# Order ties in a two-layer GLA and attention kernel: row maxima, attention set-up, prompt keys, last rows

## The chip, the cores and the metric

The kernel runs on one core of a Trainium2 chip. The metric is the device time of one execution in microseconds (us); the time before is the median of three runs, 1268.66 us (1267.31 to 1269.15).

## What is computed

Two layers of a diffusion backbone, D = 1024, on 256 prompt tokens and 1024 latent tokens. Layer 0 mixes tokens with bidirectional gated linear attention (GLA), layer 1 with grouped-query softmax attention (8 query heads, 2 key heads, head size 128). Cut to what matters here:

```
out_p, st = gla_mixer(hp, ...);  out_s, _ = gla_mixer(hs, ...)      # layer 0
xp = xp + gt_p * out_p;          xs = xs + gt_s * out_s
qp, kp, vp, gp = attn_project(hp, ...)                              # layer 1: q, k are rms-normed
out_p = (attend_blocks(qp, kp, vp) * silu(gp)) @ att_w_out          # prompt rows see prompt keys
qs, ks_ = rope_2d(qs), rope_2d(ks_)
out_s = (attend_blocks(qs, keys, vals) * silu(gs)) @ att_w_out      # latent rows: own keys and cached ones
xp = xp + gt_p * out_p;          xs = xs + gt_s * out_s
return xp, xs, gla state, prompt keys kp, prompt values vp
```

## The kernel before, in words

The 1280 tokens are ten rows of 128: rows 0 and 1 are the prompt, rows 2 to 9 the latent tokens. A product in full precision is made of three f16 products: each operand is split into a high and a low part (names hi, lo), and TensorE (PE) runs hi.hi, hi.lo and lo.hi into one PSUM bank (`pieces` and `mm3`, all at L135). Before a split the operand is scaled by a power of two that comes from its largest magnitude (`pow2`, L98 to L108: a reduction or a row maximum, then four tiny VectorE (DVE) operations).

A scheduler orders the instructions of each engine, so the code's order is not the order on the chip. `tc.issue_after(x)` ties what stands under it behind instruction x. Engines take their instructions strictly in the order so made; a wait at the head holds up all behind it.

The stages that the change touches:

- **Last GLA slots** (`filler` in the main function, slots 40 to 49). `row_load` fetches a row of GLA output from DRAM (`og_d` to `wst` or `wlo`); `row_parts` takes its maximum (L931), scales and splits it (ScalarE (ACT) L934 high part, DVE L935 low part), and a transposing DMA (L937) puts it into `hT_hi` and `hT_lo`, from which PE reads it. `row_out` makes the output row from the banks A and kt: `residual` (L916 scales the bank by the gate, L917 adds the residual row). The rows are made in the order `ROWS = (2, 3, 4, 5, 6, 7, 8, 9, 0, 1)`, the first six in the slots `EARLY = (43, 44, 45, 46, 47, 49)`. `fold_gate` loads the gate and multiplies it on GpSimd (POOL) with the weights' scales.
- **gla_out**. The last four rows (8, 9, 0, 1) are made in two banks y, and between them rows are normed (`normalise`: ACT L434 sums the squares, DVE L440 scales), transposed on PE (L445), and turned into keys and values (`key_tile`). `att_load` and `att_setup` load and scale the norm weights and the cached keys; `fill` (`out_part`) takes the attention's output weights, whose block maxima are DVE L157. Loads are issued on the SP queue.
- **key_tile** makes 128 rows of keys and values: PE product, ACT L1128 and L1131, `head_norm` (ACT L1026 twice, POOL L124 and L126, DVE L1029 twice), rotary positions for latent rows only, `split_transpose` (ACT L1056, DVE L1057, a transposing DMA L1058). For prompt rows the normed key is stored to the output cache (L1134).
- **attention**: ten steps (two key heads, five groups of 256 rows, `OUT = (1, 0, 2, 3, 4)` in the second half) of four heads each. `scores` runs PE L1180 into a tile S, takes the maximum (DVE L1183), makes its bias (ACT L1185) and the exponentials (ACT L1188), then the split (POOL L1204, DVE L1220) and a transposing DMA (L1221) to `PT`; two tiles S alternate, so that the third scores wait for the exponentials of the first. `values` multiplies with the values and the gate (DVE L1245). In the last step the first output rows are prepared.
- **att_out**: for each group of 256 rows `out2_load` fetches the gated result, `out2_scale` takes its maximum (DVE L1335 twice, L1339, PE L93, DVE L98 to L108), `out2_parts` splits it (ACT L1346, DVE L1347, in two halves of k), and `out_tile` runs two residual rows of 24 matmuls 512 wide and 48 matmuls 256 wide each (L916, L917, and a store L919). The residual row is loaded in `out_tile` (L1355).

## Time and profile before

| | |
|---|---|
| median of three runs | 1268.66 us |
| the profiled execution's own time | 1266.46 us |
| its span, first to last instruction | 1264.7 us (1.76 us lie outside) |
| mean granted TensorE clock | 0.995 |
| PE busy | 1212.7 us, 8310 matmuls |
| DVE, ACT, POOL busy | 887.0, 593.2, 402.0 us |

PE is the engine that everything else feeds. Where PE waits, the list of waits names the line that waited, the instruction that released it, the time in total, how often and the longest. A timeline row gives start, duration, engine, line, operation with output and inputs, and in square brackets the idle time of that engine just ahead of it with what ended it. A row of windows gives the busy time of PE, PEld (weight loads), DVE, ACT and POOL in a stretch, the granted PE clock (PEclk), the share of the DMA engines in use and GB/s.

### The profile page before, as it was taken

To read this page: it belongs to the slowest core of one execution; us is meant where nothing else is said; L and a number is where in the kernel's file an instruction comes from. 1 tells how busy PE (TensorE), PEld (TensorE's weight loads), DVE (VectorE), ACT (ScalarE), POOL (GpSimd) and SP (SyncE) were. 2 spreads that over 40 slices of the span, in tenths; PEclk is the share of its full clock that TensorE was granted. 3 is DMA by queue.
4 is the path that set the end of the run, shared out by engine and by line. 5 is a ranking of instruction groups with operands and counts; after the bars stand their busy time and mean duration, and the time that the engine had idled before them with its cause. 6 is when DMAs were issued, how large, how long until landed. Compare 5 with 4: busy or idle time off the path is not lost.

```text
span 1264.7 us, 22661 instructions
## 1 busy us (share of the span) xinstructions
PE 1212.7 (96%) x8310; PEld 810.4 (64%) x8310; DVE 887.0 (70%) x2040; ACT 593.2 (47%) x1439; POOL 402.0 (32%) x659
## 2 busy tenths in 40 slices
PE   5999999999999998989899989999999999999998
PEld 2448666655565556656688757767776766776665
DVE  5665886776688898763577678777658577795552
ACT  5564555555466666320255554444445355451010
POOL 0022222232233233300034645545344365533000
PEclk9999999999999999999999999999999999999999
DMA  9621365543444436893943166766938647668432
GB/s 356 208 101 35 109 196 151 188 146 113 128 124 137 129 113 215 262 207 112 333 151 118 26 163 154 137 139 134 213 80 201 141 92 149 134 159 214 163 124 93
DMA packets 335840, 194.42 MB, mean 154 GB/s; under 512 B 229662, under 2 KB 318606, under 8 KB 334448
## 3 DMA queue, kind: packets, MB, share of 16 engines
q1 hardware_dynamic: 293664, 159.02, 46.9%
q10 hardware_dynamic: 42064, 33.95, 8.3%
q8 instruction: 65, 1.06, 0.4%
q14 instruction: 47, 0.39, 0.1%
HBM read 103.00 MB, written 33.83 MB: 108 GB/s over the span
## 4 chain that ended last, share of the span: by engine, by line
PE 67%; DVE 14%; DMA 8%; ACT 4%; POOL 3%; issue 3%; SPq 0%; POOLq 0%; ACTq 0%; DVEq 0%
PE mm L135 35%; PE S L1180 7%; PE S L135 7%; PE A L135 2%; PE kt L135 2%; DVE wmx L157 2%; PE y L135 2%; DMA wst<-og_d 2%; PE kv L135 2%; PE A L750 2%; DMA wst<-in_gla_w_in 1%; DVE split L239 1%; POOL rope L1040 1%; DVE smx L1183 1%; PE A L691 1%
## 5 line engine op out<-in xcount | busy, mean ns | idle before, releaser
L135 PEld LDWEIGHTS <-hT_hi 128*128 128x128 f16 x1920 | 188.1, 98 | 133.6 <-issue 12.9
L135 PE MATMUL mm<-whi,hT_hi 128*128 128x512 f16 (+1 forms) x560 | 195.1, 349 | 4.3 <-DVE gx L280 2.5
L135 PE MATMUL mm<-whi,hT_lo 128*128 128x512 f16 (+1 forms) x560 | 195.3, 349 | 0.0
L135 PE MATMUL mm<-wlo,hT_hi 128*128 128x512 f16 (+1 forms) x560 | 195.2, 349 | 0.0
L135 PEld LDWEIGHTS <-whi 128*128 128x128 f16 x1344 | 131.3, 98 | 49.9 <-issue 2.9
L1204 POOL TENSOR_SCALAR phl<-p,srec 128x1280 f16<-128x1280 f32 (+1 forms) x80 | 105.4, 1317 | 167.8 <-DVE srec L1200 130.8
L1183 DVE TENSOR_REDUCE smx<-S 128x1 f32<-128x1280 f32 (+1 forms) x80 | 101.7, 1271 | 50.7 <-PE S L1180 50.7
L135 PEld LDWEIGHTS <-hT_lo 128*128 128x128 f16 x960 | 94.3, 98 | 62.1 <-issue 2.9
L135 PE MATMUL mm<-hT_hi,whi 128*128 128x256 f16 (+1 forms) x448 | 131.1, 293 | 0.0
L135 PE MATMUL mm<-hT_hi,wlo 128*128 128x256 f16 (+1 forms) x448 | 131.1, 293 | 0.0
L135 PE MATMUL mm<-hT_lo,whi 128*128 128x256 f16 (+1 forms) x448 | 131.0, 292 | 0.0
L1180 PE MATMUL S<-kT,wst 128*128 128x512 f16 (+1 forms) x624 | 122.1, 340 | 3.7 <-ACT p L1188 3.7
L1220 DVE SCALAR_TENSOR_TENSOR phl<-p,srec,phl 128x1280 f16<-128x1280 f32 (+1 forms) x80 | 107.6, 1345 | 15.0 <-POOL phl L1204 14.7
L135 PE MATMUL mm<-PT,vh 128*128 128x256 f16 x672 | 112.2, 273 | 1.8 <-DVE wlo L1347 1.2
L1188 ACT ACTIVATE p<-S,snb,sexp 128x1280 f32<-128x1280 f32 (+1 forms) x80 | 99.7, 1246 | 14.6 <-DVE phl L1220 5.2
L1180 PEld LDWEIGHTS <-wst 128*128 128x128 f16 x624 | 61.2, 98 | 54.8 <-issue 4.9
L135 PE MATMUL mm<-PT,vl 128*128 128x256 f16 x336 | 91.6, 273 | 0.0
L135 PEld LDWEIGHTS <-wlo 128*128 128x128 f16 x672 | 66.0, 98 | 24.3 <-issue 0.3
L1185 ACT ACTIVATE snb<-smx,nsexp 128x1 f32<-128x1 f32 x80 | 23.5, 293 | 110.1 <-DVE smx L1183 109.6
L135 PEld LDWEIGHTS <-vh 128*128 128x128 f16 x672 | 65.6, 98 | 10.5 <-issue 1.7
L1040 POOL TENSOR_TENSOR rope<-hx,ropet 128x64 f32<-128x64 f32 x160 | 66.2, 442 | 15.4 <-DVE hx L1043 10.3
L157 DVE TENSOR_REDUCE wmx<-wst 128x1 f32<-128x512 f32 x96 | 60.4, 674 | 7.4 <-DMA wst<-in_gla_w_in 7.4
(391 smaller groups left out, 2586.1 us busy)
## 6 DMA issues: line engine op xcount, KB each, us to landing
wada<-in_w_ada SPq DMA_DIRECT2D x13, 1024.0 KB
wst<-in_gla_w_in SPq DMA_DIRECT2D x12, 1024.0 KB
wst<-in_att_w_in SPq DMA_DIRECT2D x10, 1024.0 KB
xr<-x_d SPq DMA_DIRECT2D x15, 512.0 KB
og_d<-qk ACTq DMA_DIRECT2D x40, 128.0 KB
wst<-og_d SPq DMA_DIRECT2D x5, 1024.0 KB
out<-xr ACTq DMA_DIRECT2D x17, 256.0 KB
x<-in_x_sample SPq DMA_DIRECT2D x8, 512.0 KB
```

The source lines that it names most:

```text
L135: self.nc.tensor.matmul(out, a, b, start=k == 0 and j == 0, stop=k == n - 1 and j == 2)
L157: nc.vector.tensor_reduce(mx[:, j : j + 1], st[:, 2 * j : 2 * j + 2, :], AX.XY, ALU.max, apply_absolute_value=True)
L239: nc.vector.scalar_tensor_tensor(t[:, 1, v], u, s, t[:, 0, v], ALU.mult, ALU.subtract)
L691: nc.tensor.matmul(ap[:, d, :], ke[:, d, :], qe[:, d, :], start=True, stop=True)
L750: nc.tensor.matmul(o, x, y, start=j == 0, stop=j == len(terms) - 1)
L1040: nc.gpsimd.tensor_tensor(tv[:, h, :, w, :], xv[:, h, :, 1 - w, :], sn[:, :, w, :], ALU.mult)
L1180: nc.tensor.matmul(S[:, a : a + n], x, y, start=m == 0, stop=m == 2)
L1183: last = nc.vector.tensor_reduce(mx, S, AX.X, ALU.max).ins
L1185: nc.scalar.activation(nb, mx, AF.Copy, scale=self.nsexp)
L1188: nc.scalar.activation(p, S, AF.Exp, scale=self.sexp, bias=nb, accum_out=den)
L1204: nc.gpsimd.tensor_scalar(parts[:, 0:nk], p, r, 2.0 ** 14, ALU.mult, ALU.mult)
L1220: nc.vector.scalar_tensor_tensor(lo, p, r2, hi, ALU.mult, ALU.subtract)
```

## The change

It puts ties on the order at five places, and moves some work and two loads for them. Numbers of lines shift by 1 to 35 in the changed kernel (L916 and L917 become L924 and L925, L931 becomes L941, L1188 becomes L1209).

1. The maxima of rows 7, 8 and 9 stand behind the residual adds number 0, 2 and 3 (row 2 bank A, row 3 bank A, row 3 bank kt). The second half of `fold_gate` moves to slot 43.
2. The attention's set-up and the first block of output weights stand behind the last residual add of row 9.
3. A prompt row's keys stay in `qk0` after the product; their norm, store, split and transpose become `prompt_keys`, called after the first and the second scores and tied behind those scores' maxima.
4. The residual of the first output row is loaded earlier, in the last step, as two halves of 128x512 into the buffers that queries used (`hx4`), instead of one row of 128x1024 loaded in `out_tile`.
5. In `att_out` the scaling of the next group is tied behind an earlier residual add, or for the first one behind the first of the last values.

```diff
+BEHIND = {7: 0, 8: 2, 9: 3}
...
     def residual(self, i, lhs, wo, inv, x, banks=None, cuts=(512, 512), out=None):
+            xa = x[j] if isinstance(x, list) else x[:, a]
-            nc.vector.tensor_tensor(x[:, a], ps, x[:, a], ALU.add)
+            self.evac.append(nc.vector.tensor_tensor(xa, ps, xa, ALU.add).ins)
...
     def row_parts(self, i, parts):
+        n = BEHIND.get(i)
+        with nullcontext() if n is None else self.tc.issue_after(self.evac[n]):
+            mx = self.t(self.small, [P, 1], F32, "wm1")
+            nc.vector.tensor_reduce(mx, og, AX.X, ALU.max, apply_absolute_value=True)
...
-        with self.tc.issue_after(self.scaled):
+        with self.tc.issue_after(self.scaled), self.tc.issue_after(self.evac[-1]):
             self.att_setup(*ckv)
...
-        fill(0)
+        with self.tc.issue_after(self.evac[-1]):
+            fill(0)
...
     def key_tile(self, i, w):
-        x = self.t(self.hw, [P, 2, HD], F32, "hx")
+        if i < NTP:
+            x = self.qk0[:, 2048 + 256 * i : 2304 + 256 * i].rearrange("p (h d) -> p h d", h=2)
+        else:
+            x = self.t(self.hw, [P, 2, HD], F32, "hx")
-        self.head_norm(x, self.kn, x)
...
+            self.prompt.append((i, x))
         else:
+            self.head_norm(x, self.kn, x)
             self.rope(x, i)
...
+    def prompt_keys(self):
+        with self.tc.issue_after(self.last):
+            i, x = self.prompt.pop(0)
+            j = 10 + i
+            self.head_norm(x, self.kn, x)
+            self.nc.scalar.dma_start(self.O[3][0, 0, i * P : i * P + P], x)
+            self.split_transpose(x, self.asc[:, 1:2], self.kT[:, :, j * P : j * P + P])
...
                 if n == 9 and e == 0:
+                    self.first_values = None
+                    x0 = [self.t(self.hw, [P, 4, HD], F32, "hx4").rearrange("p h d -> p (h d)") for _ in range(2)]
+                    for b, t in enumerate(x0):
+                        self.nc.sync.dma_start(t, self.x1_d[2 * OUT[0], :, 512 * b : 512 * b + 512])
...
-        self.out_tile(OUT[0], 0, self.t(self.sp, [P, TS + PAST], F32, "p")[:, 0:D], wo)
+        self.out_tile(OUT[0], 0, x0, wo)
...
-                nxt = self.out2_prep(self.out2_load(OUT[n + 1]), to) if n else self.out2_parts(*self.second, to)
+                with self.tc.issue_after(self.evac[-1 - (n > 1)] if n else self.first_values):
+                    nxt = self.out2_prep(self.out2_load(OUT[n + 1]), to) if n else self.out2_parts(*self.second, to)
```

**How the order moves, place 1: DVE in the last GLA slots.** `wm` is a row's maximum, `A` and `kt` the banks of output row 3, `whi` here the buffer of its residual. Before, the maximum of row 8 and that of row 9 stand ahead of bank A's pair:

```order
L931 TENSOR_REDUCE wm_1850_7238<-wst_6294 128x1
L102 TENSOR_SCALAR p2c_7240<-wm_1850_7238 128x1
L104 TENSOR_SCALAR p2e_7242<-p2c_7240 128x1
L935 SCALAR_TENSOR_TENSOR wlo_1711_6414<-wlo_1711_6414,p2s_7101 128x1024
L106 TENSOR_SCALAR p2s_7244<-p2e_7242 128x1
L108 TENSOR_SCALAR p2i_7246<-p2e_7242 128x1
L931 TENSOR_REDUCE wm_1878_7401<-wst_6294 128x1
L916 SCALAR_TENSOR_TENSOR A_6811<-A_6811,p2i_6553,wst_6402 128x512
L98 TENSOR_REDUCE p2m_7266<-o_7264 128x1
L935 SCALAR_TENSOR_TENSOR parts_6295<-wst_6294,p2s_7244,parts_6295 128x1024
L917 TENSOR_TENSOR whi_1710_6413<-A_6811,whi_1710_6413 128x512
```

and now (what is left out are the tiny operations of row 8's scale and of the next layer's modulation):

```order
L945 SCALAR_TENSOR_TENSOR wlo_1711_6406<-wlo_1711_6406,p2s_7101 128x1024
L924 SCALAR_TENSOR_TENSOR A_6811<-A_6811,p2i_6545,wst_6402 128x512
L99 TENSOR_REDUCE p2m_7266<-o_7264 128x1
L925 TENSOR_TENSOR whi_1710_6405<-A_6811,whi_1710_6405 128x512
L941 TENSOR_REDUCE wm_1850_7238<-wst_6294 128x1
...
L945 SCALAR_TENSOR_TENSOR parts_6295<-wst_6294,p2s_7244,parts_6295 128x1024
L924 SCALAR_TENSOR_TENSOR kt_6812<-kt_6812,p2i_6545,wst_6402 128x512
L925 TENSOR_TENSOR whi_1710_6405<-kt_6812,whi_1710_6405 128x512
L941 TENSOR_REDUCE wm_1878_7401<-wst_6294 128x1
```

Both maxima have moved behind the adds that they are tied to, and the pair of bank A stands together but for one reduction.

**Place 2: DVE in gla_out, around row 9.** `y` is a bank of an output row, `xr` its residual, `st` a block of output weights, `nt` the norm's sums. Before:

```order
L1108 TENSOR_SCALAR sv_i_7905<-inv_av_7902 128x1
L124 TENSOR_SCALAR nt_r2a_7638<-nt_s_1928_7635 128x2
L440 TENSOR_SCALAR xr_7616<-xr_7616,nt_r_1930_7640 128x1024
L440 TENSOR_SCALAR xr_7618<-xr_7618,nt_r_1930_7640 128x1024
L916 SCALAR_TENSOR_TENSOR y_7670<-y_7670,p2i_7246,wst_6402 128x512
L157 TENSOR_REDUCE wmx_7992<-st_7632 128x1
L124 TENSOR_SCALAR nt_r2a_7780<-nt_s_1947_7777 128x2
L157 TENSOR_REDUCE wmx_7992<-st_7632 128x1 x3
L917 TENSOR_TENSOR xr_7620<-y_7670,xr_7620 128x512
```

and now:

```order
L1119 TENSOR_SCALAR sv_i_7905<-inv_av_7902 128x1
L125 TENSOR_SCALAR nt_r2a_7638<-nt_s_1928_7635 128x2
L924 SCALAR_TENSOR_TENSOR y_7670<-y_7670,p2i_7246,wst_6402 128x512
L441 TENSOR_SCALAR xr_7616<-xr_7616,nt_r_1930_7640 128x1024
L441 TENSOR_SCALAR xr_7618<-xr_7618,nt_r_1930_7640 128x1024
L925 TENSOR_TENSOR xr_7620<-y_7670,xr_7620 128x512
L125 TENSOR_SCALAR nt_r2a_7780<-nt_s_1947_7777 128x2
L441 TENSOR_SCALAR xr_7622<-xr_7622,nt_r_1949_7782 128x1024
L441 TENSOR_SCALAR xr_7624<-xr_7624,nt_r_1949_7782 128x1024
```

The four L157 left the space between the pair of bank y (now L924 and L925).

**Place 3: ACT from the last prompt keys to the first exponentials.** `hx` before and `qk` now hold the prompt row's keys, `xhl` their split, `p` the exponentials. Before:

```order
L1128 ACTIVATE hx_9268<-kv_9219,inv_k_7900 128x256
L1131 ACTIVATE vh_7898<-kv_9219,psv_7908 128x256
L1134 DMA out<-hx_9197 128x256
L1056 ACTIVATE xhl_9215<-hx_9197,asc_7890 128x256
L1026 ACTIVATE hjunk_9271,hssq_9270<-hx_9268 128x128
L1136 ACTIVATE pv_2188_9283<-kv_9219,inv_av_7902 128x256
L1026 ACTIVATE hjunk_9271,hssq_9270<-hx_9268 128x128
L1137 DMA out<-pv_2188_9283 128x256
L1134 DMA out<-hx_9268 128x256
L1056 ACTIVATE xhl_9286<-hx_9268,asc_7890 128x256
L1185 ACTIVATE snb_9329<-smx_9327,nsexp_7894 128x1
L1188 ACTIVATE p_9331,sden_9332<-S_9309,snb_9329,sexp_7892 128x1280
```

and now:

```order
L1142 ACTIVATE qk_7_82<-kv_9203,inv_k_7900 128x256
L1144 ACTIVATE vh_7898<-kv_9203,psv_7908 128x256
L1148 ACTIVATE pv_2177_9255<-kv_9203,inv_av_7902 128x256
L1149 DMA out<-pv_2177_9255 128x256
L1206 ACTIVATE snb_9297<-smx_9295,nsexp_7894 128x1
L1209 ACTIVATE p_9299,sden_9300<-S_9277,snb_9297,sexp_7892 128x1280
L1170 ACTIVATE hx_2191_9308<-mm_9309,inv_q_1977_7928 128x256
L1170 ACTIVATE hx_2191_9308<-mm_9309,inv_q_1978_7930 128x256
...
L1037 ACTIVATE hjunk_9383,hssq_9382<-qk_7_82 128x128 x2
...
L1206 ACTIVATE snb_9369<-smx_9367,nsexp_7894 128x1
L1209 ACTIVATE p_9371,sden_9372<-S_9357,snb_9369,sexp_7892 128x1280
```

The norm's sums (L1037, four of them on `qk`) and the splits moved from ahead of the first exponentials (L1209) to behind them; the sums on `qk` stand ahead of the second ones.

On SP, the 1 MB load `whi<-w_q` of the first query weights now stands right behind the first two loads of `w_kv` and ahead of the six loads `xr`; before it stood behind the transposes of row 0 (`parts`). One of the two 0.5 MB loads `wkv` goes the other way.

More of the change, by code (lines that the diff above doesn't have):

```diff
@@ L894, in gla, with fold_gate @@
                 w = nw
-    def fold_gate(self, l, inv, gt):
+    def fold_gate(self, l, inv, gt, later=False):
         nc = self.nc
@@ L901, in fold_gate, with fold_rest @@
             nc.sync.dma_start(gt[:, i, :], self.gt_d[l, i : i + 1, :].to_broadcast([P, D]))
+        if later:
+            return
+        self.fold_rest(inv)
+    def fold_rest(self, inv):
+        nc, gt = self.nc, self.gt
         for b in range(4):
@@ L975, in gla_out @@
                 nc.sync.dma_start(w[part], d[:, part, :, 256 * j : 256 * j + 256])
-        self.o1 = []
+        self.o1, self.prompt = [], []
         fill = self.out_part(2, self.kept2)
@@ L1298, in attention @@
                     self.query_rest()
+                if self.prompt:
+                    self.prompt_keys()
                 if len(pend) == 2:
@@ L1354, in out_tile @@
         i, a = 2 * c + j, slice(j * P, j * P + P)
-        self.nc.sync.dma_start(x, self.x1_d[i])
+        if not isinstance(x, list):
+            self.nc.sync.dma_start(x, self.x1_d[i])
         S = self.t(self.ps, [P, 1536], F32, "S")
@@ L1556, in emit @@
         wo, part, held, rows, parts, xs, waiting = [None] * 4, [], [], [], [], [], []
+        inv_wo = None
         def filler(slot):
+            nonlocal inv_wo
             if part:
@@ L1599, in filler @@
                 gt = k.t(k.wst, [P, KT, 256], F32, "wst").rearrange("p (i k) n -> p i (k n)", i=2)
-                k.fold_gate(0, [t[2] for t in wo], gt)
+                inv_wo = [t[2] for t in wo]
+                k.fold_gate(0, inv_wo, gt, True)
                 wo[:] = [(*k.w0[0:2], 512)] + [(hi, lo, 256) for hi, lo, _ in wo[2:]]
+            if slot == EARLY[0]:
+                k.fold_rest(inv_wo)
             n = slot - LATE
```

13 lines of the change are left out of this document (5 added, 8 removed).

## The prediction

> **What bounds the kernel now.** I read the page first, then the list of PE's waits, then timelines at each place.
>
> ```profile
> PE 1212.7 (96%) x8310; PEld 810.4 (64%) x8310; DVE 887.0 (70%) x2040; ACT 593.2 (47%) x1439; POOL 402.0 (32%) x659
> PE A L135 <- DVE p2c L102: 3.9, 1, 3.9
> PE y L135 <- DVE xr L917: 2.8, 1, 2.8
> PE S L1180 <- ACT p L1188: 2.7, 1, 2.7
> ...
> PE tr L445 <- DVE xr L440: 0.6, 1, 0.6
> ...
> PE S L135 <- DVE p L917: 1.7, 2, 1.1
> PE mm L135 <- DVE wlo L1347: 1.2, 1, 1.2
> ```
>
> PE is busy 96% of the span, so only its idle time can be won, and of that the second half of the program holds the rows above (the first four from 500 to 800 us, the last two from 1100 to the end). The profile's clock shows a second cost behind the long ones; the rows are the stretches behind the first three waits:
>
> ```profile
> 555.00:560.00 5.00, 1.06 (x7) 0.54 (x5) 4.49 (x14) 0.00 (x0) 0.00 (x0) 0.90 1.11 295
> 560.00:565.00 5.00, 5.00 (x20) 1.95 (x18) 2.88 (x6) 1.15 (x1) 0.00 (x0) 0.76 1.13 252
> ...
> 625.00:630.00 5.00, 3.03 (x16) 2.22 (x17) 5.00 (x14) 1.02 (x2) 1.19 (x3) 0.72 1.11 260
> 630.00:635.00 5.00, 5.00 (x43) 4.20 (x42) 1.91 (x5) 1.02 (x2) 1.07 (x2) 0.93 0.82 292
> ...
> 740.00:745.00 5.00, 5.00 (x31) 3.59 (x30) 3.80 (x7) 3.30 (x11) 4.67 (x9) 0.67 0.36 82
> ```
>
> Over ten us behind the first wait the granted clock misses (0.10 + 0.24) x 5 = 1.7 us, behind the second (0.28 + 0.07) x 5 = 1.75, behind the third 0.33 x 5 = 1.65. Some of that falls on idle time, so I count 1.5 for each. The 1.1 to 1.2 us waits at the end show no such dip.
>
> **Place 1, the row maxima.** DVE in the last GLA slots:
>
> ```profile
> 550.29 1.22 DVE L931 TENSOR_REDUCE wm<-wst 128x1 f32<-128x1024 f32 x1 [2.05 <-DMA wst<-og_d]
> ...
> 555.51 1.22 DVE L931 TENSOR_REDUCE wm<-wst 128x1 f32<-128x1024 f32 x1 [2.29 <-DMA wst<-og_d]
> 556.64 0.75 DVE L916 SCALAR_TENSOR_TENSOR A<-A,p2i,wst 128x512 f32<-128x512 f32 x1
> 557.50 1.27 DVE L935 SCALAR_TENSOR_TENSOR parts<-wst,p2s,parts 128x1024 f16<-128x1024 f32 x1
> 558.69 0.68 DVE L917 TENSOR_TENSOR whi<-A,whi 128x512 f32<-128x512 f32 x1
> ```
>
> PE waits 3.9 us for bank A of row 3. The maximum of row 9 (555.51) waits 2.29 us for its load in front of the pair L916, L917, although the bank needs neither, and the low part at 557.50 stands between the two. In the new order the low part of row 7 (1.27) comes where the maximum of row 8 stood: from about 550 to 551.3, then L916 with the reduction (0.86, from 556.64 to 557.50) and L917 (0.68) end near 552.8. PE got the bank when L917 ended, at 559.4, so it wanted it at 559.4 - 3.9 = 555.5: this wait goes. What is late next is bank kt, wanted 24 matmuls of 512 columns later. At place 4 rows show 24 matmuls of 256 columns in 2.61 us (0.109 each, so 0.215 for twice the width): at 560.7. Ahead of its pair stand the maximum of row 8 (1.22, to 554.0), its scale (0.9, the time from L98 to L1346 in the rows of place 5), ACT's high part (1.1, half of that L1346) and the low part (1.27), so the pair ends near 558.8; if the row's load is 2 us later than at 550.29, no later than 560.8. Removed 3.9 + 1.5 = 5.4; I keep 0.2 for kt: **-5.2** (bounds -3.9 if the dip comes from elsewhere, -5.4). The maxima of rows 8 and 9 come some 3 us later; the products of rows 4 to 7 lie between them and their use. Moving the second half of the gate's multiplication costs nothing: it is POOL work with no wait on it in the list.
>
> **Place 2, set-up behind row 9.**
>
> ```profile
> 618.44 1.06 ACT L434 ACTIVATE junk<-xr 128x1024 f16<-128x1024 f32 x1 [12.22 <-DMA hT_lo<-parts]
> ...
> 623.78 0.68 DVE L157 TENSOR_REDUCE wmx<-st 128x1 f32<-128x512 f32 x1
> 624.44 1.87 DVE L157 TENSOR_REDUCE wmx<-st 128x1 f32<-128x512 f32 x3
> 626.23 0.68 DVE L917 TENSOR_TENSOR xr<-y,xr 128x512 f32<-128x512 f32 x1
> ...
> 605.00:610.00 5.00, 5.00 (x36) 3.24 (x34) 2.70 (x4) 1.15 (x1) 0.00 (x0) 1.00 1.03 395
> ```
>
> PE waits 2.8 us (with 0.6 just before, for L440) for the L917 at 626.23; four maxima L157 (0.68 + 1.87) stand between the pair. Without them the pair would end near 623.8. Both chains begin with ACT's sums at 618.44, which waited 12.22 us for a transpose to land: four times 1.2 us later DVE may scale (L440). There the change puts a load of 1 MB ahead and takes 0.5 MB away, on DMA engines that are full (share 1.03, 395 GB/s): 0.5 MB at that rate is 1.3 us. So the sums start near 619.7, the L440 end near 624.5 and the L917 near 625.2. PE, in the new order, has all of row 9's first half (24 matmuls instead of 20) ahead of the transposes that need L440; before, it came to these some 5 us ahead of 626.9, the L917's end, near 621.9, so now near 622.7. It then waits some 1.2 + 0.5 + 0.5 us in pieces too short for a dip: 2.2 us. Removed 2.8 + 0.6 + 1.5 = 4.9, added 2.2: **-2.7** (bounds: -4.9 with the load harmless, +0.5 with the whole MB ahead, 2.6 us, and the dip back). The L157 come later; the list of waits has no row of PE on their result.
>
> **Place 3, prompt keys behind the first scores.**
>
> ```profile
> 730.01 0.49 DVE L1132 SCALAR_TENSOR_TENSOR vl<-kv,psv,vh 128x256 f16<-128x256 f32 x1
> 732.97 0.61 DVE L1029 SCALAR_TENSOR_TENSOR hx<-hx,hrs,kn 128x128 f32<-128x128 f32 x2 [1.52 <-POOL hrs L126]
> 733.50 1.48 DVE L1183 TENSOR_REDUCE smx<-S 128x1 f32<-128x1280 f32 x1
> ...
> 737.33 0.48 DVE L1057 SCALAR_TENSOR_TENSOR xhl<-hx,asc,xhl 128x256 f16<-128x256 f32 x1 [2.35 <-ACT xhl L1056]
> 736.79 0.51 ACT L1056 ACTIVATE xhl<-hx,asc 128x256 f16<-128x256 f32 x1 [4.91 <-DMA wst<-xhl]
> 737.52 1.42 ACT L1188 ACTIVATE p<-S,snb,sexp 128x1280 f32<-128x1280 f32 x1
> 751.32 0.38 PE L135 MATMUL mm<-whi,hT_hi 128*128 128x512 f16 x1 [0.85 <-DVE gx L280]
> 746.38 1.42 POOL L1204 TENSOR_SCALAR phl<-p,srec 128x1280 f16<-128x1280 f32 x1 [1.11 <-DVE srec L1200]
> 746.64 1.44 DVE L1043 TENSOR_TENSOR hx<-hx,rope 128x256 f32<-128x256 f32 x1
> ...
> 745.00:750.00 5.00, 5.00 (x37) 3.33 (x35) 5.00 (x7) 2.77 (x6) 3.46 (x5) 1.00 0.23 52
> ```
>
> ACT stands 4.91 us at the split of the second prompt key, which waits for a buffer that a transpose still reads; the first exponentials (737.52) are queued behind it, and the third scores wait 2.7 us for these. In the new order DVE starts the first maximum when the values' low part is done, near 730.5; 1.48 for it, 1.42 for the exponentials and about 0.5 for the short ACT steps around them (an estimate: 0.2 from the end of L1056 to 737.52, twice and a bit) bring these to 733.9. The third scores then find a free tile. With the dip (1.5) and the 0.85 at 751.32 the most that can go is 2.7 + 1.5 + 0.85 = 5.0.
>
> But the prompt keys' work does not vanish: two times 0.61 + 0.48 = 2.2 us move on DVE into the stretch from 745, where it is busy 5.00 of 5.00 us, and somewhat more on ACT, which has 2.2 us free there (2.77 busy). What DVE gets on top comes off the gain as long as DVE sets the pace: 5.0 - 2.2 = 2.8, **-2.8** (bounds -5.0, if DVE's waits for POOL take it up, and 0, if as much again is lost on ACT). The transposes of the prompt keys go behind those of `PT` on SP; only the prompt group's scores, the last step of the first half, need them. The two halves of `w_q` that SP now issues ahead of a transpose have 24 matmuls, 5.2 us, until the second scores.
>
> Here a rule speaks against the change. POOL's L1204 at 746.38 lasts 1.42, and DVE's L1043 at 746.64 lasts 1.44 and ends 0.28 after it; L1057, on as many elements, takes 0.48. The Trainium skill (SBUF — State Buffer, section "SBUF: two separate sides") says that a DVE operation with two SBUF inputs and a GpSimd operation that reads SBUF lock each other out for a whole instruction; by that rule, which this pair of rows agrees with, each of the moved operations can lose up to one L1204 of 1.42. With one such hold-up place 3 would give -1.4 in place of -2.8, inside my bounds.
>
> **Place 4, the first output row's residual.**
>
> ```profile
> 1151.86 0.38 PE L135 MATMUL mm<-PT,vh 128*128 128x256 f16 x2
> 1154.47 0.38 PE L135 MATMUL mm<-PT,vh 128*128 128x256 f16 x2
> ...
> 1154.53 0.75 DVE L916 SCALAR_TENSOR_TENSOR S<-S,p2i,wst 128x512 f32<-128x512 f32 x1
> 1161.33 0.69 DVE L917 TENSOR_TENSOR p<-S,p 128x512 f32<-128x512 f32 x1 [1.20 <-DMA p<-x_d]
> ```
>
> Before, the last values wait 1.2 us and the second half of the first output row 0.6 us, the latter for the residual row that lands at 1161.33. With the row there early, the second half (48 matmuls of 0.109, 5.2 us) moves in front of the last values, and their transposes are then long there. But it needs L917 of the first half. DVE has L916 only at 1154.53; with the reduction 0.86, and L917 0.69, it ends at 1156.1 or a little later. PE is through with its 25 matmuls of values at 1154.6. So a new wait of 1.6 us replaces 1.86: **-0.3** (bounds -1.9, +0.5).
>
> **Place 5, scaling in the output stage.**
>
> ```profile
> 1172.07 0.28 DVE L98 TENSOR_REDUCE p2m<-mm 128x1 f32<-128x128 f32 x1
> 1172.95 2.19 ACT L1346 ACTIVATE whi<-wst,p2s 128x1024 f16<-128x1024 f32 x2 [14.70 <-DVE p2s L106]
> 1177.24 0.32 SPq L1325 DMA_DIRECT2D wst<-og_d  x1
> 1183.25 2.35 DVE L1335 TENSOR_REDUCE wmx<-wst 128x1 f32<-128x1024 f32 x2 [4.64 <-DMA wst<-og_d]
> ```
>
> The wait of 1.1 us (at 1171, L917 behind two maxima that waited for their load) goes. New: the scaling comes later against PE. PE starts the third group's first row 14 matmuls (3.0 us) after the spread L93; it needs the scale (about 0.9), one L1346 (2.19 / 2 = 1.1) and for its third matmul one L1347 (1.27, as L935 on as many elements): 3.3 us against 3.0 + 0.43. I put 0.1 to 0.2 at each of three groups: 0.4 in all, **-0.7** (bounds -1.1, +2).
>
> **The sum.** -5.2 - 2.7 - 2.8 - 0.3 - 0.7 = -11.7. Against the profiled execution (a span of 1264.7 and 1.76 outside it, 1266.46) that is 1254.8; its time lies 2.2 under the median of the runs, so the forecast is 1268.66 - 11.7 = **1257.0**. A difference under 0.2%, 2.5 us, is about what this measurement cannot tell from none.
>
> **The rivals.**
>
> A. *DMA and DVE take back places 2 and 3.* The full DMA engines delay the sums by 2.6 us, and DVE's full stretch keeps PE's pace in place 3. For it: share 1.03, DVE 5.00 of 5.00. Against: PE idles at exactly those two waits. Then -5.2 - 0 - 0 - 1.0 = -6.2: 1262.5. Chance 0.20.
>
> B. *The dip has another cause than the wait.* The slow stretches at places 2 and 3 stay when the waits of 2.8 and 2.7 us go; place 1 keeps its gain. Then -11.7 + 2 x 1.5 = -8.7: 1260.0. Against: each dip starts within the same five us as its wait. Chance 0.04. The Trainium skill (TensorE: Matmul & The Clock Gate, Part 1) has the clock halved only after an idle window of about 3.4 us; only the wait of 3.9 reaches that, so by the page B would hold, and the rows, which show dips behind 2.7 and 2.8, speak against it.
>
> C. *Nothing: the waits come back one stage on.* PE that is early at 560 meets loads and transposes that are not early. For it: the full DMA engines from 605 on. Against: the stores and loads ahead of place 2 are issued as PE's rows come out, so they come earlier too. -2 to 0: about 1267.7. Chance 0.10.
>
> D. *Slower: the output stage.* The load of group n+1 may go only when both L1347 of group n are done. In the rows it takes 6.0 us (1177.24 to 1183.25), then 2.35 for the maxima and 0.9 + 1.1 + 1.27 for the scale and the split: 11.6 us, against two rows of 10.4 us each (24 x 0.215 + 48 x 0.109), 20.8. In the new order the maxima stand behind a first half's pair, and L93 in the middle of the next matmuls, so a load that lands more than about 6 us later than in the rows stops PE, at three groups. If each then loses a first half, 24 matmuls of 0.215 = 5.2, that is +15.6 - 11.7 = +3.9: 1272.6. It decides from loads of 12 us on. Against: the load would have to take twice the time of the rows. Chance 0.06.
>
> **Chances and range.** My forecast 0.60, A 0.20, B 0.04, C 0.10, D 0.06. Faster by over 0.2% are forecast, A and B: 0.84; within it C: 0.10; slower D: 0.06. The forecast's own range goes from all terms at their better bound (-5.4 - 4.9 - 5.0 - 1.9 - 1.1 = -18.3: 1250.4) to half of what places 2 and 3 give (-8.9: 1259.7). To hold 8 in 10 the range takes in A, with the bound of +2 at place 5 counted in part, and B: 1250 to 1264.
>
> **What would show it.** Right: in the list of waits A <- p2c and S <- p L1209 (L1188 before) from 500 to 800 us are gone, y <- xr is split in waits under 1.3 us, PEclk is 1.00 from 555 to 565 and from 740 to 745; near 1155 one new wait of S on DVE of 1.3 to 1.8. Wrong: PEclk under 0.8 near 630 (A), waits of S on `wlo` or `wm` after 1190 (D), or PE waits on the maxima's successors from 745 to 770 of over 3 us (A at place 3).

## The result and the profile after

The changed kernel takes 1255.76 us in the median of four runs (1254.37 to 1258.98) beside 1268.91 us (1267.31 to 1269.97) for the kernel before: a ratio of 0.9901, with a 95% interval of 0.9877 to 0.9925. A second comparison gave 1255.13 us against 1266.37, ratio 0.9918 [0.9902, 0.9934]; one of the eleven runs of the kernel before in it took 5532.85 us at a granted clock of 0.218 and is left out of the ratio. About 1% faster, as forecast; the forecast was 1257.0. The profiled execution of the changed kernel took 1254.37 us, with a span of 1252.6.

The busy line of the page:

```profile
PE 1205.8 (96%) x8310; PEld 809.2 (65%) x8310; DVE 886.1 (71%) x2040; ACT 593.9 (47%) x1439; POOL 408.1 (33%) x659
```

The work is the same (8310 matmuls on PE); PE is busy 6.9 us less (1212.7 before). Most of that is the clock: from 400 us on, before has four stretches at half clock (behind waits that end at 530.4, 559.4, 627.0 and 739.1 us), which cost 1.7 + 1.5 + 1.7 + 1.7 = 6.6 us, and the changed kernel has one (at 632.9), 1.6 us. The list of PE's waits from 500 to 800 us, its four longest rows, and the first row of the list from 1100 us to the end (line that waited, instruction waited for, total us, times, longest):

```profile
PE kv L94 <- DVE amx L1091: 4.5, 1, 4.5
PE mm L136 <- DVE gx L281: 3.5, 2, 1.8
PE A L136 <- DMA hT_hi<-parts: 1.8, 1, 1.8
PE S L1201 <- ACT p L1209: 0.7, 1, 0.7
...
PE S L136 <- DVE p2c L103: 2.0, 1, 2.0
```

The waits of 3.9, 2.8 and 2.7 us of before are gone or down to 0.7. At the top stands one that the prediction did not have: PE waits 4.5 us for the ×16 step of the set-up's maxima. The windows that answer to the prediction's five:

```profile
555.00:560.00 5.00, 5.00 (x40) 3.72 (x39) 3.69 (x8) 1.15 (x1) 0.00 (x0) 1.00 1.08 284
560.00:565.00 5.00, 5.00 (x35) 3.27 (x34) 2.46 (x4) 0.00 (x0) 0.00 (x0) 1.00 1.10 208
625.00:630.00 5.00, 3.42 (x27) 2.48 (x25) 1.00 (x2) 0.56 (x1) 0.40 (x1) 1.00 1.02 400
630.00:635.00 5.00, 2.12 (x11) 1.56 (x12) 4.97 (x13) 1.60 (x3) 0.40 (x1) 0.76 0.32 129
635.00:640.00 5.00, 5.00 (x41) 4.06 (x40) 3.92 (x21) 3.65 (x7) 0.81 (x2) 0.90 0.02 5
740.00:745.00 5.00, 5.00 (x25) 2.27 (x24) 4.95 (x9) 2.29 (x4) 0.79 (x2) 1.00 0.81 184
```

PE is full and at full clock from 555 to 565, and at full clock from 740 to 745. The dip near 630 is still there, behind another wait: the granted clock of 0.76 is what the prediction named as its sign of rival A (under 0.8 near 630), but the cause is another one, as the experiments show.

**Where the time went, by stages.** Three matmuls, named o, y and S after the banks that they write, exist in all kernels of this study and cut the last 700 us into stages. Their rows are, first before the change and then after it:

```profile
548.93 0.22 PE L93 MATMUL o<-ident,af_m 128*128 128x128 bf16 x1
...
607.13 0.38 PE L135 MATMUL y<-whi,hT_hi 128*128 128x512 f16 x1
...
727.28 1.03 PE L1180 MATMUL S<-kT,wst 128*128 128x512 f16 x4
```

```profile
545.64 0.22 PE L94 MATMUL o<-ident,af_m 128*128 128x128 bf16 x1
...
598.29 0.38 PE L136 MATMUL y<-whi,hT_hi 128*128 128x512 f16 x1
...
718.17 1.79 PE L1201 MATMUL S<-kT,wst 128*128 128x512 f16 x9
```

The stage from o to y holds place 1, from y to S place 2 (and the work ahead of place 3's first scores), from S to the end of the span places 3, 4 and 5. All times in us, from the profiled execution of each kernel; the median is that of its runs:

| kernel | median | o to y | y to S | S to end | o to end |
|---|---|---|---|---|---|
| before | 1268.91 | 58.20 | 120.15 | 537.42 | 715.77 |
| changed | 1255.76 | 52.65 | 119.88 | 534.43 | 706.96 |
| changed, second time | 1255.13 | 52.65 | 119.85 | 534.35 | 706.85 |
| e1, place 1 undone | 1262.05 | 58.83 | 120.00 | 534.79 | 713.62 |
| row 9's tie alone at place 1 | 1258.90 | 52.65 | 122.64 | 533.66 | 708.95 |
| e2, place 2 undone | 1255.23 | 52.65 | 119.72 | 534.41 | 706.78 |
| e3, place 3 undone | 1260.59 | 52.66 | 120.45 | 537.48 | 710.59 |
| e4, places 4 and 5 undone | 1258.73 | 52.65 | 121.14 | 536.44 | 710.23 |
| place 4 undone | 1258.70 | 52.65 | 122.51 | 536.11 | 711.27 |
| place 5 undone | 1256.17 | 52.65 | 120.08 | 532.14 | 704.87 |
| maxima behind the ×16 step | 1251.88 | 52.65 | 118.36 | 531.93 | 702.94 |
| cached loads first | 1257.04 | 52.65 | 120.77 | 533.77 | 707.19 |
| both | 1251.42 | 52.65 | 115.76 | 532.73 | 701.14 |
| ×16 step, no tie on the set-up | 1253.94 | 52.65 | 119.90 | 534.89 | 707.44 |

From o to end the changed kernel is 8.8 us shorter: 5.55 at place 1, 0.3 in place 2's stage, 3.0 behind it. The remaining 3.3 us of the difference of the spans (1264.7 - 1252.6 = 12.1) lie ahead of o, at 548.93 and 545.64, where the orders differ in little. In the ten other profiles that have the changed kernel's edits up to there o comes at 545.96 to 549.96; the 548.93 of before lies within that. So this part goes with the execution, and no effect of the change is shown in it. Some 2.2 of the 3.3 us are one wait, that of bank A for the transpose into `hT_hi` near 530 us: 2.27 us and a dip of 1.7 before, 1.83 without a dip after; in the other profiles the same wait is 1.0 to 2.6 us long. The table also tells what a stage is good for. From o to y it repeats within 0.02 us in 12 profiles. The longer stages do not: where the experiment meant to touch nothing, y to S reaches 122.51 (place 4 undone) beside 119.88, and S to end lies between 531.93 and 534.89.

The last stage can be cut once more, at the matmuls of the last head's scores, which wait 0.4 to 0.5 us for exponentials in every kernel. Before and after:

```profile
1135.40 0.81 PE L1180 MATMUL S<-kT,wst 128*128 128x512 f16 x3 [0.46 <-ACT p L1188]
```

```profile
1124.48 1.78 PE L1201 MATMUL S<-kT,wst 128*128 128x512 f16 x9 [0.40 <-ACT p L1209]
```

From S to there, where place 3 acts, it is 408.12 us before and 406.31 in the changed kernel (404.39 to 406.47 in the eleven other profiles with place 3 in, 409.29 in e3 with place 3 undone). From there to the end of the span, where places 4 and 5 act, it is 129.30 before and 128.12 in the changed kernel (127.54 to 129.83 in the nine others with both places in, 130.70 with place 4 undone, 127.14 with place 5 undone, 131.43 with both undone). So place 3 gave 1.8 us in this pair of profiles and places 4 and 5 together 1.2.

The theory after the result: place 1 and place 3 work as forecast, place 2 exchanges a wait for another of its size, and the ends (places 4, 5) give about the 1.0 forecast. The rival: the gains lie elsewhere (DMA traffic, fewer dips by chance) and the single ties are worth nothing by themselves.

### The profile page after: what moved, and what is told of

Read it like the earlier page. It is cut to its first block, busy times and chain, and to the rows that moved or that the text cites. A ratio compares the mean times of both kernels' runs of the same rounds, so it can differ in the third digit from the quotient of the medians.

```text
span 1252.6 us, 22659 instructions
## 1 busy us (share of the span) xinstructions
PE 1205.8 (96%) x8310; PEld 809.2 (65%) x8310; DVE 886.1 (71%) x2040; ACT 593.9 (47%) x1439; POOL 408.1 (33%) x659
## 5 line engine op out<-in xcount | busy, mean ns | idle before, releaser
L1209 ACT ACTIVATE p<-S,snb,sexp 128x1280 f32<-128x1280 f32 (+1 forms) x80 | 99.7, 1246 | 15.0 <-DVE phl L1241 6.2
L1206 ACT ACTIVATE snb<-smx,nsexp 128x1 f32<-128x1 f32 x80 | 23.5, 293 | 110.3 <-DVE smx L1204 109.8
L158 DVE TENSOR_REDUCE wmx<-wst 128x1 f32<-128x512 f32 x96 | 60.4, 674 | 6.7 <-DMA wst<-in_gla_w_in 6.7
```

Of the source, the lines that this page charges most:

```text
L158: nc.vector.tensor_reduce(mx[:, j : j + 1], st[:, 2 * j : 2 * j + 2, :], AX.XY, ALU.max, apply_absolute_value=True)
L1206: nc.scalar.activation(nb, mx, AF.Copy, scale=self.nsexp)
L1209: nc.scalar.activation(p, S, AF.Exp, scale=self.sexp, bias=nb, accum_out=den)
```

## The experiments

Each experiment ran beside the kernel before, on one of three chips; only on one of them (row 9's tie alone, and the first two of the four kernels at the end) did the changed kernel run as well. Where e1 to e4, places 4 and 5 alone and the last two kernels are set against 1255.13 to 1255.76 us, the comparison goes across chips, on which the kernel before had 1267.0, 1266.37 and 1267.47 us.

**e1: place 1 alone undone.**

```diff
-BEHIND = {7: 0, 8: 2, 9: 3}
+BEHIND = {}
```

> The changed kernel without place 1: the maxima of rows 7, 8 and 9 are no longer tied behind the residual adds (BEHIND is empty); all else as changed. Theory T (each place read at landmarks of the two traces): the wait of 3.9 us for bank A and the dip of PE's clock behind it come back, so 5 to 6 us over the changed kernel, near 1261.3, and in the trace A <- p2c of over 3 us with a PEclk under 0.9 in one of the two stretches of five us behind it. Rival R (the 3.3 us that the changed kernel's trace is ahead of before already at 545 us belong to the change too, by the DMA order around the rows): 8 to 9 us, near 1264.5. Rival N (the time came from elsewhere): under 2 us.

Measured: 1262.05 us, ratio to before 0.9968 [0.9947, 0.9988], 6.2 us more in the stage from o to y and under 0.4 in the others; 6.3 to 6.9 us above the changed kernel in the medians. Theory T held, a little low; R and N did not. The list of waits of this kernel has the old wait back:

```profile
PE A L136 <- DVE p2c L103: 4.3, 1, 4.3
```

and its windows have the dip behind it:

```profile
555.00:560.00 5.00, 1.93 (x6) 0.78 (x6) 4.80 (x18) 1.15 (x1) 0.00 (x0) 0.84 1.11 289
560.00:565.00 5.00, 5.00 (x21) 2.03 (x19) 1.73 (x2) 0.00 (x0) 0.00 (x0) 0.81 1.10 236
```

So place 1 is worth 5.5 to 6.2 us: a wait of 4 us, and the dip of the clock behind it, (0.16 + 0.19) x 5 = 1.75 us. VectorE's rows show the same queue as before:

```profile
554.14 1.22 DVE L941 TENSOR_REDUCE wm<-wst 128x1 f32<-128x1024 f32 x1 [2.13 <-DMA wst<-og_d]
555.28 0.75 DVE L924 SCALAR_TENSOR_TENSOR A<-A,p2i,wst 128x512 f32<-128x512 f32 x1
```

The maximum stands idle 2.13 us for its load, with the pair that PE needs behind it.

**Row 9's tie alone.**

```diff
-BEHIND = {7: 0, 8: 2, 9: 3}
+BEHIND = {9: 3}
```

> Of the first place's three ties (rows 7, 8 and 9) only row 9's is kept, so that rows 7 and 8 have their maximum where the order had it before the change. Theory (of the 4.3 to 5 us that TensorE lost there, it lost nearly all on row 9's maximum, which stood in front of the steps that it waited for): the time is within 1 us of the changed kernel's, no wait of TensorE above 1 us between 545 and 565 us, granted clock 1.00 there. Rival (rows 7 and 8 keep VectorE 1.4 us late, and the lateness is carried to row 9's place): 2 to 6 us slower than the changed kernel, with a wait of 2 us or more on p2c near 552 us.

Measured: the stage from o to y is 52.65 us, exactly that of the changed kernel, and no wait for p2c near 552. All of place 1 is row 9's tie; the ties of rows 7 and 8 give nothing there. The time, 1258.90 us, is still 3.8 above the changed kernel's on the same chip, beyond the 1 us expected: the stage from y to S is 2.8 longer, and the wait for `amx` 5.4 us instead of 4.4. Whether rows 7 and 8 matter for that wait was not settled: with place 4 alone undone, which changes nothing meant for this stage, it is 2.7 us longer too, so the 2.8 are no more than the stage moves by itself.

**e2: place 2 alone undone.**

```diff
-        with self.tc.issue_after(self.scaled), self.tc.issue_after(self.evac[-1]):
+        with self.tc.issue_after(self.scaled):
             self.att_setup
...
-        with self.tc.issue_after(self.evac[-1]):
-            fill(0)
+        fill(0)
```

> The changed kernel without place 2: neither the attention's set-up nor the first block of output weights is tied behind row 9's last residual add. Theory T (a wait was exchanged: y <- xr of 2.8 us and its dip went, and PE now stands 4.5 us at the spread of the set-up's maxima, with a dip): within 1.5 us of the changed kernel, 1254.3 to 1257.3, with y <- xr of 2 us or more back and the wait of kv on amx gone. Rival P (the prediction's term for place 2): 2.7 us slower than the changed kernel, near 1258.5.

Measured: 1255.23 us, ratio 0.9916 [0.9889, 0.9943]; y to S is 119.72 us against 119.88. With the other places in, place 2 is worth nothing. The theory's time held, but neither of the two waits that it named did as expected (2 us or more for `xr`, none for `amx`):

```profile
PE kv L94 <- DVE amx L1090: 2.0, 1, 2.0
...
PE y L136 <- DVE xr L925: 0.5, 1, 0.5
```

VectorE's rows show why:

```profile
616.83 0.68 DVE L925 TENSOR_TENSOR xr<-y,xr 128x512 f32<-128x512 f32 x1
...
620.23 2.47 DVE L158 TENSOR_REDUCE wmx<-st 128x1 f32<-128x512 f32 x4 [2.64 <-DMA st<-in_att_w_out]
```

The scheduler, freed of the tie, did not put the four block maxima back between the pair of bank y, as in the kernel before; they stand behind it and wait 2.64 us for their load. So the edit takes out the ties but does not restore the old order, and the 2.8 us wait for `xr` of before does not come back: it is 0.5. In its stead PE waits 2.0 for the set-up's maxima even here, with a granted clock of 0.66 from 625 to 630. The two ties exchange this wait and some short ones for one of 4.5.

**e3: place 3 alone undone.** The prompt keys' norm, store, split and transpose go back into the function that makes them (its core):

```diff
-        if i < NTP:
-            x = self.qk0[:, 2048 + 256 * i : 2304 + 256 * i].rearrange("p (h d) -> p h d", h=2)
-        else:
-            x = self.t(self.hw, [P, 2, HD], F32, "hx")
+        x = self.t(self.hw, [P, 2, HD], F32, "hx")
...
+        self.head_norm(x, self.kn, x)
...
-                if self.prompt:
-                    self.prompt_keys()
```

> The changed kernel without place 3: the prompt keys' norm, store and split stand in key_tile again, ahead of the first scores. Theory T (landmarks): 2.4 us slower, near 1258.2, with S <- p L1209 of over 2 us and PEclk near 0.7 behind it. Rival A (DVE sets the pace there, so that the wait only moves): within 1 us of the changed kernel. Rival M (all of the wait, the dip and the later wait goes): 5 us slower, 1260.8.

Measured: 1260.59 us, ratio 0.9954 [0.9935, 0.9972]; S to end is 3.1 us longer than in the changed kernel, y to S 0.6. The median is 4.8 to 5.5 us above the changed kernel's, so by the runs rival M (1260.8) came nearer than theory T (1258.2); the trace has 3.7 of it from y on. In the list of waits S L1198 <- ACT p L1206 is back with 2.6 us, and the granted clock from 735 to 740 is 0.66. The queue that makes it, ScalarE:

```profile
729.99 0.51 ACT L1067 ACTIVATE xhl<-hx,asc 128x256 f16<-128x256 f32 x1 [2.08 <-DMA wst<-xhl]
...
733.31 0.51 ACT L1067 ACTIVATE xhl<-hx,asc 128x256 f16<-128x256 f32 x1 [0.57 <-DMA wst<-xhl]
733.73 1.40 ACT L1206 ACTIVATE p<-S,snb,sexp 128x1280 f32<-128x1280 f32 x1
```

The exponentials stand behind both splits of the prompt keys again. Right ahead of them the queue waits only 0.57 us, not 4.91; but the first split had waited 2.08 us for a transpose, VectorE's low part of that key stood behind it and the first scores' maximum (730.93) behind that, and ScalarE waited 1.95 us for this maximum (its bias, L1203, at 732.45). The scores' wait is as long as before.

**e4: places 4 and 5 undone together, and each alone.** The first edit (place 4) and the second (place 5):

```diff
-                    x0 = [self.t(self.hw, [P, 4, HD], F32, "hx4").rearrange("p h d -> p (h d)") for _ in range(2)]
-                    for b, t in enumerate(x0):
-                        self.nc.sync.dma_start(t, self.x1_d[2 * OUT[0], :, 512 * b : 512 * b + 512])
...
-        self.out_tile(OUT[0], 0, x0, wo)
+        self.out_tile(OUT[0], 0, self.t(self.sp, [P, TS + PAST], F32, "p")[:, 0:D], wo)
...
-                with self.tc.issue_after(self.evac[-1 - (n > 1)] if n else self.first_values):
+                if True:
```

> The changed kernel without places 4 and 5: the first output row's residual is loaded in out_tile again, and the output stage's scaling is not tied. Theory T (prediction's terms -0.3 and -0.7, landmarks -1.2): 1 us slower, near 1256.8; at the end three waits of PE of 1.1, 0.6 and 1.2 us in place of one of 2.0. Rival D (the later scaling costs PE): faster than the changed kernel by 1 us or more.

> Place 4 alone undone: the first output row's residual goes back into the wide buffer it shared with the scores' copies. Taking out places 4 and 5 together cost 3.0 us of the median and 3.3 us behind 545 us in the trace, where the prediction had 0.3 and 0.7. Theory (most of it is place 4: the load of that row waits for the buffer, and the matmuls at the change from attention to the outputs wait for it): 2 to 3 us slower than the changed kernel, with waits on xr or p, L925, and on PT near 1155 us. Rival (place 4 is worth the 0.3 us that was predicted): within 1 us of the changed kernel, no new wait above 0.6 us.

> Place 5 alone undone: the loads and the set-up of the next output stage stand where they stood before. Theory (if place 4 carries most of the 3 us): within 1 us of the changed kernel, with one wait of about 1.6 us on wm, L1364, and a part of it made up behind. Rival (place 5 carries it): 2 to 3 us slower, the wait on wm at its full 1.6 us and a dip of the granted clock or a second wait behind it. If both runs come out at under 1 us, the two ties are worth 3 us only together.

Measured: together 1258.73 us, ratio 0.9943 [0.9925, 0.9962]; place 4 alone 1258.70, 0.9938 [0.9921, 0.9956]; place 5 alone 1256.17, 0.9916 [0.9899, 0.9933]. Against the changed kernel's 1255.13 to 1255.76 both undone cost 3.0 to 3.6 us and not the 1 of theory T; place 4 alone costs as much, and place 5's is within 1 us of nothing. With place 4 undone the list of waits from 1100 us on is

```profile
PE mm L136 <- DMA PT<-phl: 3.0, 1, 3.0
...
PE S L136 <- DVE p L925: 0.4, 1, 0.4
```

and the windows around the longest of them are

```profile
1150.00:1155.00 5.00, 1.99 (x10) 0.76 (x9) 2.98 (x5) 2.19 (x2) 0.00 (x0) 0.94 1.15 297
1155.00:1160.00 5.00, 5.00 (x34) 3.91 (x33) 0.69 (x1) 0.00 (x0) 0.00 (x0) 0.72 0.81 273
```

The last values stand 3.0 us for the transpose of the last scores, and a dip of (0.06 + 0.28) x 5 = 1.7 us follows. In the changed kernel the first output row's matmuls lie there instead, and one wait of 2.0 us is left, without a dip: 3.0 + 1.7 + 0.4 - 2.0 = 3.1, about what the runs give. From the last scores to the end the trace has 2.6 of it (130.70 against 128.12; 0.9 to 3.2 against all profiles with place 4 in). Another 2.6 us of this profile lie in y to S, where place 4 does nothing; how much of the 3 us of the medians is of that kind was not settled. Place 5 undone showed neither a wait on `wm` above 1 us nor a longer stage. The wait of 1.6 us on `wm` (L1364) is in the kernel that has both undone.

**The changed kernel a second time.** Unaltered, as the measure for the next kernels on their chip.

> The changed kernel once more, unaltered, so that the three kernels beside it have it on their own chip. If the comparison of the medians holds (0.9901, 1255.8 us), the time is 1253 to 1258 us and the ratio 0.988 to 0.993. If a part of the first difference was the luck of one chip, the ratio is above 0.993. The trace should again show one wait of TensorE of 4 to 5 us on the set-up's maxima near 630 us (L94 on amx, L1091), two of 1 to 2 us on gx and no other above 1 us between 500 and 800 us; if that wait is not there, it was an accident of one execution and not of the order.

Measured: 1255.13 us; all three stages within 0.1 us of the first profile, the wait for `amx` 4.4 us. Of the two waits for gx one is 1.7 us and one 0.8, and the one for `hT_hi` near 531, which was not named, is 1.9. The new wait belongs to the order, not to one execution.

**What the wait of 4.5 us is.** VectorE's rows in the changed kernel around it, PE's row, and SP's issues of the loads:

```profile
622.43 0.27 DVE L1090 TENSOR_REDUCE amx<-kn 128x1 f32<-128x128 f32 x1
629.00 1.37 DVE L1093 TENSOR_REDUCE amx<-hx 128x1 f32<-128x512 f32 x2 [6.30 <-DMA hx<-in_cache_k]
630.29 2.46 DVE L158 TENSOR_REDUCE wmx<-st 128x1 f32<-128x512 f32 x4
632.67 0.16 DVE L1091 TENSOR_SCALAR amx<-amx 128x2 f32<-128x2 f32 x1
...
632.88 0.29 PE L94 MATMUL kv<-ident,amx 128*128 128x128 bf16 x1 [4.46 <-DVE amx L1091]
...
622.68 0.34 SPq L250 DMA_DIRECT2D wlo<-w_q  x1
623.11 0.46 SPq L1082 DMA_DIRECT2D hx<-in_cache_k  x1
```

L1091 multiplies the two norms' maxima by 16; its input is there at 622.7 (L1090). It runs at 632.67, because in VectorE's queue it stands behind the maxima of the cached keys, idle 6.30 us for a load issued at 623.11, and behind the four block maxima L158, 2.46 us. In the kernel before, the same step and the cached maximum stood the other way round:

```profile
629.62 0.15 DVE L1080 TENSOR_SCALAR amx<-amx 128x2 f32<-128x2 f32 x1
...
636.40 0.69 DVE L1082 TENSOR_REDUCE amx<-hx 128x1 f32<-128x512 f32 x1 [0.80 <-DMA hx<-in_cache_k]
```

Four kernels test this.

**The cached maxima behind the ×16 step.**

```diff
-        nc.vector.tensor_scalar(m[:, 0:2], m[:, 0:2], 16.0, None, ALU.mult)
+        x16 = nc.vector.tensor_scalar(m[:, 0:2], m[:, 0:2], 16.0, None, ALU.mult).ins
...
+            with self.tc.issue_after(x16):
                 nc.vector.tensor_reduce(
```

> The two maxima over the cached keys and values are tied behind the step that multiplies the two norms' maxima by 16, so that this step no longer stands behind a wait for the cached keys' load. Theory (the wait of 4.46 us near 630 us is one of order in VectorE's queue: the step's input is there at 622.7 us and it ran at 632.7): the wait on the first of the four transposes goes or falls below 1 us; the three others come 2.6 us later and need the cached maxima, which VectorE now has at about the same time as before, so up to 1 us of wait may stay there. Gain 2.5 to 5 us against the changed kernel: 1251 to 1254 us on a chip where that one has 1256. Rival 1 (TensorE waits for the data of the cached loads whatever the order): the wait moves to the other three transposes at full length, and the time stays within 1 us. Rival 2 (nothing but the weights' maxima, four times 0.6 us, holds the step): the same 4.5 us stays, since they still stand ahead of it.

Measured: 1251.88 us, ratio 0.9893 [0.9875, 0.9911], 3.3 us below the changed kernel on the same chip; its four runs, 1250.79 to 1254.27, overlap with the other's five (1254.22 to 1257.22) by 0.05 us. VectorE's rows and PE's:

```profile
626.86 0.16 DVE L1091 TENSOR_SCALAR amx<-amx 128x2 f32<-128x2 f32 x1
631.50 1.37 DVE L1094 TENSOR_REDUCE amx<-hx 128x1 f32<-128x512 f32 x2 [4.47 <-DMA hx<-in_cache_k]
...
633.73 0.34 PE L94 MATMUL kv<-ident,amx 128*128 128x128 bf16 x3 [2.73 <-DVE amx L1097]
```

The first transpose no longer waits. The other three, which need the cached maxima, do, 2.73 us rather than the "up to 1 us" expected, and a dip follows (0.70 from 635 to 640). The order was the cause of a part, the late load of the rest. From y to S, where the edit acts, 1.5 us are gained; the other 2.5 us of the profile lie behind S, where it changes nothing that was meant, and are as much as that stage moves by itself. So the 3.3 us of the medians are not all shown to be the tie's.

**The cached loads ahead of the queries' weights.**

```diff
-        with self.tc.issue_after(self.scaled):
+        with self.tc.issue_after(self.scaled), self.tc.issue_after(self.cached):
             self.wq = [self.load_w("q0", 2)]
```

> The loads of the first queries' weights are tied behind the loads of the cached keys and values on SyncE, so that the cached keys' load is issued some 5 us earlier than at 623.1 us. Theory (the step behind the wait is held by the late issue of that load, which stood behind a weights load that waited 5.4 us for its buffer): VectorE has the cached keys by 624 to 625 us, the wait of TensorE near 630 us falls from 4.5 us to under 2, and the kernel gains 2.5 to 5 us against the changed one; the weights behind it are not needed before 700 us and cost nothing. Rival (the loads are limited by their buffers or by the traffic and not by the place in the queue): the load lands at 628 to 629 us as before and the time stays within 1 us.

Measured: 1257.04 us, ratio 0.9934 [0.9917, 0.9951]: 1.9 us slower than the changed kernel on the same chip, the intervals of the two ratios overlapping. The wait near 630 is gone, as expected. PE comes to the 72 matmuls for the last bank y 61.63 us behind the landmark y, the changed kernel's profile on this chip 68.83 (at 661.89 and 670.03 us). Some 3 of these 7 us are only order: 7 matmuls of the queries' product, 512 wide, stand ahead of that point and not 22. The lead is lost before S. The waits from 640 to 730 us:

```profile
PE kv L136 <- POOL hT_hi L468: 1.1, 3, 0.7
PE kv L136 <- DVE hT_lo L469: 1.1, 2, 0.6
```

The windows there:

```profile
710.00:715.00 5.00, 3.54 (x24) 2.03 (x22) 3.35 (x9) 1.91 (x9) 4.68 (x12) 0.90 0.21 47
715.00:720.00 5.00, 5.00 (x37) 3.96 (x35) 3.23 (x9) 1.64 (x5) 1.63 (x5) 0.75 1.15 244
```

PE, early, runs into the producers of `hT` (POOL L468 and DVE L469), the activations of the last rows, which are not early: 2.2 us in five short waits close together, and a dip of (0.10 + 0.25) x 5 = 1.75 us though none of the five is above 0.7 us.

**Both.**

> Both orders at once: the cached keys' loads ahead of the queries' weights, and the cached maxima behind the step by 16. With the first alone TensorE's wait near 630 us went altogether and its lead of 5 to 7 us was lost at 708 to 718 us to four waits on hT_hi and hT_lo (2.2 us) and a stretch of half clock; with the second alone 3.2 us were gained and kept. Theory (the producers of hT, at work without a pause through 640 to 715 us, set the earliest end of this stage, some 3 us below the changed kernel): as the first alone, no wait near 630 us, waits at 708 to 715 us, and a time between 1251 and 1257 us, not below the second alone. Rival (the two gains add): 1249 us or less, no waits at 708 to 715 us.

Measured: 1251.42 us, ratio 0.9878 [0.9859, 0.9898], the best of the study and, within the runs, equal to the kernel with the ×16 tie alone (1251.88). y to S is 115.76 us, the shortest; no wait near 630 and one of 0.4 on `hT_lo` at 712. So the theory put on record, that the producers of hT set a floor which returns the waits, fell, though its time range (1251 to 1257 us) was met and the rival's 1249 us was not: the same lead ends in 2.2 us of waits in one kernel and in 0.4 in the other. The two differ by one tie and by the order that the scheduler made around it; what in it counts was not isolated.

**The ×16 tie without the tie on the set-up.** The set-up's instructions and loads stand where they did without place 2's first tie.

> The cached maxima behind the step by 16, and the tie of the attention's set-up taken out, so that the set-up's loads are issued as early as before the change. Theory (the wait near 630 us has two causes in VectorE's queue, the place of the step and the late loads, and this one takes both away while the queries' weights keep their place): the wait on amx falls to under 1 us, the time is 1250 to 1254 us. Rival (as with the cached loads put first, what is gained is lost at 708 to 718 us to the producers of hT): waits of 2 us there, 1254 to 1258 us.

Measured: 1253.94 us, ratio 0.9897 [0.9879, 0.9915]. No wait on `amx`; one of 1.6 on `xr` (L925) near 631 and one of 1.0 for a weights load came in its place, and o to end is 707.44 us against 706.96. Again an exchange.

## Why the prediction was right, and where not

The direction was right, and the time came close: 1255.76 for 1257.0. The mechanisms of places 1, 3, 4 and 5 are in the trace. Place 2's term failed, place 3's was met in part, and the stages that the change touches give 8.8 us of the 11.7. That the time was met all the same is in part luck: 3.3 us of the profiled difference lie where no effect of the change is shown.

**Place 1, -5.2: right.** 5.55 us in the stage's length, 6.2 when undone. The order forecast is in VectorE's rows:

```profile
548.23 0.75 DVE L924 SCALAR_TENSOR_TENSOR A<-A,p2i,wst 128x512 f32<-128x512 f32 x1
...
549.09 0.68 DVE L925 TENSOR_TENSOR whi<-A,whi 128x512 f32<-128x512 f32 x1
...
554.71 0.69 DVE L925 TENSOR_TENSOR whi<-kt,whi 128x512 f32<-128x512 f32 x1
555.32 1.21 DVE L941 TENSOR_REDUCE wm<-wst 128x1 f32<-128x1024 f32 x1
```

The maximum of row 9 stands behind the pair of kt and waits for nothing. No wait on kt was left, so the 0.2 kept for it was not needed. Not foreseen: one tie of the three carries it all.

**Place 2, -2.7: wrong, -0.3.** Two steps failed. "The L157 come later; the list of waits has no row of PE on their result" looked at the list of before, where nothing waited for what stood behind the block maxima: the ×16 step ran at 629.62, and PE came to its result only at 634.32. The term put the set-up that moved with the tie at nothing. Nothing was asked about who stands behind the moved instructions in VectorE's queue in the new order. The second, the delay of the sums by the load of 1 MB, did not happen:

```profile
609.13 1.06 ACT L435 ACTIVATE junk<-xr 128x1024 f16<-128x1024 f32 x1 [11.76 <-DMA hT_lo<-parts]
```

609.13 against 618.44 is 9.3 us earlier, where PE itself is 8.8 earlier (y at 598.29 and 607.13). So in the changed kernel all of 2.8 + 0.6 + 1.5 = 4.9 is gone, and the wait of 4.5 with its dip took it back. Even the removal is not all the ties' doing: with them undone and the other places in, the wait for `xr` is 0.5. This is rival A's outcome at place 2, for none of rival A's reasons: the DMA engines delayed nothing here, an instruction at the head of a queue did. (In the prediction's working the pair without the maxima ends near 624.4 and not 623.8, where its first half ends, and VectorE may scale the first two rows after two of the four sums, at 621.79; no term hangs on either.)

**Place 3, -2.8: right in kind, 1.8 in size.** The stretch from S to the last scores is 1.8 us shorter than before; the other profiles with place 3 in it are 1.7 to 3.7 shorter. Undone it costs 3.1 us from S to end in the trace. The exponentials were to be done at 733.9 on the time axis of before. They start at 724.80 and end at 726.22; at S this execution is 727.28 - 718.17 = 9.11 earlier, so that is 735.3, against 738.9 before: 1.4 later than forecast. The maximum ahead of them began at 722.95 (732.06), not at 730.5, since the low part of the values that it stands behind came later too (722.55, which is 731.66, against 730.01). It was early enough: the third scores wait for nothing.

```profile
724.80 1.42 ACT L1209 ACTIVATE p<-S,snb,sexp 128x1280 f32<-128x1280 f32 x1
```

The reserve of 2.2 us for VectorE's added work shows as a wait of 1.76 for gx, where before had 0.85, and one of 0.69 of later scores; in the second profile of the same kernel the wait for gx is 0.82, so 0.7 to 1.6 us are shown of it, and the 0.85 that the term counted as gain did not go. The rule of the Trainium skill (SBUF — State Buffer, section "SBUF: two separate sides") that would have made it -1.4 took nothing extra: of the moved instructions none lasts over 0.73 us, and one rotation step (L1054) lasts 1.34 where others take 0.42, as one did before.

**Places 4 and 5, -0.3 and -0.7: right, -1.2 together.** The new wait of 1.6 us forecast is there with 2.0:

```profile
1145.85 2.78 PE L136 MATMUL S<-kept,ropet 128*128 128x256 f16 x24 [2.03 <-DVE p2c L103]
```

It replaces 1.2 + 0.6 us, so place 4 gave about nothing, and the wait of 1.1 that place 5 was to take away is gone. From the last scores to the end the changed kernel is 1.2 us shorter than before. What no term said is what place 4 is worth beside the other places: undone there, it does not bring back the 1.2 and 0.6 of before but a wait of 3.0 with a dip of 1.7. Place 5 undone shows no loss in the runs (within 1 us) and none in the trace.

**The sum.** -5.55 - 0.3 - 1.8 - 1.2 = -8.8 from o to end, against -11.7. The runs differ by 13.15 and 11.2 us; 3.3 us of the profiled pair's 12.1 lie ahead of o. What makes the medians differ by some 2 to 4 us more than the stages was not settled. **The rivals:** B fell, since every dip went with its wait; C and D did not come, and no wait on `wlo` or `wm` follows 1190 us in the changed kernel.

## What to carry to other kernels

A tie that moves a reduction with a late load moves a blockage: list, in the new order, every cheap instruction that now stands behind it in the same queue, and who waits for that. A list of waits of the old kernel cannot show these. A piece can be worth more beside the other pieces than against the old kernel, and a tie taken out need not restore the old order: read the order that came out. Measure a short stage between two fixed matmuls rather than the whole: one of 53 us repeated within 0.02 us here, while stages of 120 and 530 us moved by some 3 and whole runs of one kernel spread over 3 to 11.
